# FFN input product by Strassen's method in 18 of 22 pairs, with running sums of the output in DRAM

## The chip, the cores and the metric

One core of a Trainium2 chip runs the whole kernel. The metric is the time of one execution on the device in microseconds; the median of three runs is given, and the profile is of one further execution.

## The reference

An encoder block on 1024 tokens of width 1024: a projection feeds an attention branch and a state-space branch, they are merged, and a gated FFN follows. Only the FFN matters here:

```python
h = _rms(x, g_pre_ffn[l]) * (1.0 + sc2) + sh2
g, up = jnp.split(h @ w_ffn_in[l], 2, axis=-1)
f = (jax.nn.silu(g) * up) @ w_ffn_out[l]
x = x + gt2 * _rms(f, g_post_ffn[l])
```

The hidden width is 2816, which is 22 tiles of 128. `sh2`, `sc2` and `gt2` come from a vector `c` through a 1024x6144 matrix.

## The kernel before, in words

Data lie with channels on the 128 partitions and tokens along the free axis, in two halves of 512 tokens. Products are kept near float32 accuracy by splitting both operands into a high part (fp32r, a cast on ScalarE) and a low part (a subtraction on VectorE); `mm3` (L197) then makes three matmuls for each 128x128 block of weights: high by high, high by low, low by high. Instructions stand on each engine in the order in which the program emits them.

A pair is one tile of 128 hidden channels: its gate columns and its up columns of the input weights. `ffn_in` (L1599) gets both weight tiles (128x1024, 8 blocks of k), makes for each half two sums of 8 x 3 matmuls of 512 columns, so 96 a pair over both halves, then Silu on ScalarE, a multiplication on VectorE, and the split of the result into `fhi` and `flo`. `ffn_out` (L1616) makes one output tile (128 channels by one half, m of 8) from the pairs of one group: 3 matmuls a pair, then adds PSUM to the running sum `facc` (tile `mr`), which stays in SBUF. `FGROUPS` (L31) gives the pairs of each group, 4, 4, 4, 4, 3 and 3. The first and the last group run half by half, so that work for the other half can lie beside them; the others run both halves for each weight tile.

`WStream` (L150) issues weight loads on SyncE (L166) in the order of use, at most two raw tiles, and splits them one tile ahead of the use (`get`, L188). `prod` (L1477) calls `tick` every other k, which emits one step of a generator from `backlog`: the norm of the other half in `chain` (L1531) before the FFN, and `final` (L1628), which after the last sums norms them, adds the residual and stores the result. `ada_load` and `ada_do` (L927, L937) load rows of the 6144-column matrix and reduce each with one VectorE operation of 128x1024 (L455); eight of these, for the last gate, stand in the FFN loop (L1666), one in attention at step 2. The last output half is made in quarters of 256 columns. `ps_b` (L1372) gives one of 8 PSUM banks.

A DMA is issued by an instruction on the queue of SyncE, ScalarE or GpSimd. Where its target or source buffer is still in use, that instruction waits, and what is behind it on the queue waits too.

## Time and profile before

| | |
|---|---|
| median of 3 runs | 1685.14 us (1682.86 to 1685.48) |
| profiled execution | 1684.47 us |
| its span, first to last instruction | 1682.7 us |
| mean granted clock of TensorE | 0.983 |
| busy: TensorE / VectorE / ScalarE / GpSimd | 1618.4 / 977.7 / 552.5 / 164.0 us |
| moved by DMA | 189.66 MB |

The FFN begins near 930 us and lasts to the end. Busy time of TensorE is modelled, and its matmuls overlap: the time that one costs is read from the starts of a run of them. "Idle before" gives what a waiting instruction was released by. Timeline rows give start, duration, engine, line, operation and tile; "x2" after a row means that so many of a kind were merged.

### The profile page before, as it was taken

Reading aid. Unit: us, or ns where it says so; the run is one execution under the profiler, and the core shown is the slowest. Engines: PE = TensorE matmul, PEld = TensorE weight load, DVE = VectorE, ACT = ScalarE, POOL = GpSimd, SP = SyncE. Lnnn points to the kernel's source line nnn. Section 1 sums busy time; section 2 is a strip of 40 time slices with the busy share of each in tenths; the row PEclk is TensorE's granted clock in tenths of the full one; section 3 lists DMA queues with packets and bytes.
Section 4 is the critical chain, followed back from the end, with each engine's and each line's share of the span. In section 5 each row is a group of like instructions: output and inputs, shape, how many; then the busy total and the mean of one; then the engine's idle time right before and its main releaser. Section 6 shows DMA issues by size and latency. Waiting matters only on the chain.

```text
span 1682.7 us, 19415 instructions
## 1 busy us (share of the span) xinstructions
PE 1618.4 (96%) x7454; PEld 1309.0 (78%) x7454; DVE 977.7 (58%) x1615; ACT 552.5 (33%) x743; POOL 164.0 (10%) x221
## 2 busy tenths in 40 slices
PE   6989999999899999999999999999999999999995
PEld 6878888888688677767777778888888888888874
DVE  6978898977857778854636763223223222323366
ACT  4142322223531467763334443211111121121233
POOL 0430000012220000000524200000000000000002
PEclk9899999999999999999999999999999999999998
DMA  8143333567987424202523442212111111111243
GB/s 330 63 124 100 108 103 94 157 218 221 310 244 223 104 63 101 45 14 67 196 94 107 162 135 91 73 66 79 59 63 51 50 51 50 51 41 48 80 142 129
DMA packets 90748, 189.66 MB, mean 113 GB/s; under 512 B 19992, under 2 KB 36504, under 8 KB 90656
## 3 DMA queue, kind: packets, MB, share of 16 engines
q1 hardware_dynamic: 57920, 120.62, 23.7%
q10 hardware_dynamic: 27104, 49.95, 8.6%
q0 software_dynamic: 5632, 17.86, 3.5%
q8 instruction: 58, 0.95, 0.2%
q14 instruction: 34, 0.28, 0.1%
HBM read 148.61 MB, written 39.78 MB: 112 GB/s over the span
## 4 chain that ended last, share of the span: by engine, by line
PE 65%; DVE 20%; ACT 5%; DMA 4%; issue 4%; ACTq 1%; SPq 0%; DVEq 0%; POOLq 0%
PE mm L203 17%; PE mm L202 17%; PE mm L201 17%; DVE t L66 5%; DVE wlo L66 2%; PE sc L1255 1%; PE sc L1256 1%; PE sc L1257 1%; PE pv L1281 1%; PE pv L1280 1%; PE pv L1282 1%; ACT whi L183 1%; DMA mxd<-mneg 1%; PE mx L1203 1%; DVE s L695 1%
## 5 line engine op out<-in xcount | busy, mean ns | idle before, releaser
L202 PE MATMUL mm<-mh,whi 128*128 128x512 f32 x736 | 289.3, 393 | 4.8 <-DVE mh L74 3.1
L201 PE MATMUL mm<-mh,whi 128*128 128x512 f32 x736 | 289.8, 394 | 0.8 <-ACT mh L1404 0.5
L203 PE MATMUL mm<-mh,wlo 128*128 128x512 f32 x736 | 288.7, 392 | 1.7 <-DVE wlo L66 1.6
L66 DVE TENSOR_TENSOR wlo<-wraw,whi 128x1024 fp32r<-128x1024 f32 (+1 forms) x128 | 155.8, 1235 | 80.2 <-ACT whi L183 80.1
L66 DVE TENSOR_TENSOR silu<-mm,silu 128x512 f32<-128x512 f32 x44 | 30.4, 692 | 277.4 <-PE mm L203 271.2
L183 ACT CAST whi<-wraw 128x1024 fp32r<-128x1024 f32 (+1 forms) x128 | 129.9, 1036 | 149.0 <-PE mm L202 137.0
L202 PEld LDWEIGHTS mm<-mh,whi 128*128 128x128 f32 x736 | 139.2, 189 | 38.2 <-DVE mh L74 6.6
L203 PEld LDWEIGHTS mm<-mh,wlo 128*128 128x128 f32 x736 | 139.2, 189 | 32.9 <-DVE wlo L66 4.3
L201 PEld LDWEIGHTS mm<-mh,whi 128*128 128x128 f32 x736 | 139.2, 189 | 31.1 <-ACT whi L183 0.9
L201 PE MATMUL mm<-hhi,whi 128*128 128x512 f32 x384 | 156.7, 408 | 1.5 <-ACT ev L604 1.5
L202 PE MATMUL mm<-hlo,whi 128*128 128x512 f32 x384 | 152.8, 398 | 1.4 <-DVE hlo L74 1.4
L203 PE MATMUL mm<-hhi,wlo 128*128 128x512 f32 x384 | 153.5, 400 | 0.0
L201 PE MATMUL mm<-fhi,whi 128*128 128x512 f32 x304 | 118.8, 391 | 0.0
L202 PE MATMUL mm<-flo,whi 128*128 128x512 f32 x304 | 118.5, 390 | 0.0
L203 PE MATMUL mm<-fhi,wlo 128*128 128x512 f32 x304 | 118.3, 389 | 0.0
L66 DVE TENSOR_TENSOR mr<-mm,mr 128x512 f32<-128x512 f32 (+1 forms) x88 | 56.3, 641 | 97.1 <-PE mm L203 97.0
L66 DVE TENSOR_TENSOR plo<-p,phi 128x1024 fp32r<-128x1024 f32 x64 | 78.3, 1224 | 40.0 <-ACT phi L1261 39.6
L1613 ACT CAST fhi<-silu 128x512 fp32r<-128x512 f32 x44 | 27.3, 621 | 222.2 <-DVE silu L66 222.2
L201 PEld LDWEIGHTS mm<-hhi,whi 128*128 128x128 f32 x384 | 73.3, 191 | 19.6 <-ACT ev L604 1.9
L202 PEld LDWEIGHTS mm<-hlo,whi 128*128 128x128 f32 x384 | 73.1, 190 | 18.5 <-DVE hlo L74 1.8
L1260 ACT ACTIVATE p<-sc 128x1024 f32<-128x1024 f32 x64 | 65.7, 1026 | 64.5 <-PE sc L1257 64.5
L203 PEld LDWEIGHTS mm<-hhi,wlo 128*128 128x128 f32 x384 | 73.0, 190 | 17.9 <-DVE wlo L66 0.2
(524 smaller groups left out, 2938.7 us busy)
## 6 DMA issues: line engine op xcount, KB each, us to landing
wraw<-in_wfi SPq DMA_DIRECT2D x58, 512.0 KB
wraw<-in_win SPq DMA_DIRECT2D x26, 512.0 KB
wraw<-in_wfo SPq DMA_DIRECT2D x20, 512.0 KB
gdram<-ev ACTq DMA_DIRECT2D x32, 256.0 KB
wada<-in_wada POOLq DMA_DIRECT2D x15, 512.0 KB, 4.3
wraw<-in_wmix SPq DMA_DIRECT2D x10, 512.0 KB
xT<-in_xT SPq DMA_DIRECT2D x8, 512.0 KB
pw<-in_wadk SPq DMA_DIRECT2D x8, 512.0 KB
```

The source lines that it names most:

```text
L66: return self.eng.tensor_tensor(o, a, b, op=op)
L183: A_.copy(hi, t)
L201: PE.matmul(ps, whi[:, c], rhi, start=first, stop=False)
L202: PE.matmul(ps, whi[:, c], rlo, start=False, stop=False)
L203: PE.matmul(ps, wlo[:, c], rhi, start=False, stop=last)
L695: V.tensor_tensor_scan(t[64:P, 511::-1], r[64:P, ::-1], z[i][64:P, ::-1], 0.0, op0=ALU.mult, op1=ALU.add)
L1203: PE.matmul(pieces[j], qt["qhi"][b][0:96, t * P:(t + 1) * P], qt["khi"][b][0:96, halves[j]], start=True, stop=True)
L1255: PE.matmul(ps[:, c], kh[0:97, kc], qh[0:97, c], start=True, stop=False)
L1256: PE.matmul(ps[:, c], kh[0:96, kc], ql[0:96, c], start=False, stop=False)
L1257: PE.matmul(ps[:, c], kl[0:96, kc], qh[0:96, c], start=False, stop=True)
L1260: A_.activation(p, ps, AF.Exp)
L1613: A_.copy(fh[:, c], t)
```

## The change

The gate and up weights of a pair and the two halves of k form a 2x2 matrix of blocks, and the two halves of k and of the tokens another. From pair 4 on, `pair7` makes their product from 7 products of blocks (4 blocks of k by 512 tokens, so 4 x 3 = 12 matmuls each) where 8 were made, with sums of blocks on both sides. The sums of the token side (T1 to T4) are made and split once, in steps from `backlog` (`tops_12`, `tops_4`, `tops_3`); those of the weights are made for each pair by three or four GpSimd operations, and all seven weight blocks are split (`Blocks`). `Blocks.load` issues weight loads on GpSimd's queue, and `Blocks.get` has blocks split three ahead of the use.

Groups become 4, then seven of 2, then 4 pairs. Group 0 runs half by half as before with the old product. Running sums live in a DRAM tensor `fd` [2, 8, 128, 512]: `f_load` brings one tile of 256 KB into one of four buffers `fio`, `ffn_out` adds PSUM to it and stores it back, both on SyncE. In groups 1 to 7 the load of the tile three further on is emitted ahead of the tile itself. The last group makes its sums into SBUF, half 0 and then half 1 in quarters. The eight late reductions move from the FFN to steps 50 to 59 of attention.

```diff
-FGROUPS = [4, 4, 4, 4, 3, 3]
+FGROUPS = [4, 2, 2, 2, 2, 2, 2, 2, 4]
+AHEAD = 3
...
+            ada_do()
+        if 50 <= i < 60:
+            ada_do()
+            ada_load(1, ap, "wada", 2)
...
     ff_es = ExitStack()
-    fp = pool("fp", stack=ff_es)
+    fp = pool("fp", bufs=2, stack=ff_es)
+    mhc = pool("mhc", stack=ff_es)
+    fd = dram.tile([2, KD, P, HF], F32, name="fd")
...
+    def f_load(h, m, c0=0, n=HF):
+        t = f_tile()[:, 0:n]
+        SY.dma_start(t, fd[h, m][:, c0:c0 + n])
+        fio.append(t)
+
+    def ffn_out(g, m, h, w, off, c0=0, n=HF):
         ps = ps_b()[:, 0:n]
-        tiles = ft_group[g]
         c = slice(h * HF + c0, h * HF + c0 + n)
-        prod(ps, w, lambda k: tiles[k][0][:, c], lambda k: tiles[k][1][:, c], FGROUPS[g], m % 2 * FGROUPS[g])
-        r = facc[h][:, m, c0:c0 + n]
-        if g == 0:
+        tiles = [ft[p] for p in range(starts[g], starts[g + 1])]
+        prod(ps, w, lambda k: tiles[k][0][:, c], lambda k: tiles[k][1][:, c], FGROUPS[g], off)
+        if g == last:
+            r = facc[h][:, m, c0:c0 + n]
+            tt(r, ps, fio.pop(0), ALU.add)
+            return r
+        if g:
+            r = fio.pop(0)
+            tt(r, ps, r, ALU.add)
+        else:
+            r = f_tile()
             A_.copy(r, ps)
-        else:
-            tt(r, ps, r, ALU.add)
-        return r
...
+    class Blocks:
+
+
+        def __init__(self, seq):
+            self.seq, self.n, self.got, self.raw, self.hl = seq, 0, 0, [], []
+            self.loads = []
+            for kind, i, j in seq:
+                if kind == "A11":
+                    self.loads += [a["wfi"][2 * i], a["wfi"][2 * i + 1]]
+                elif kind == "O" and j % 2 == 0:
+                    o = 2 * starts[i] * P
+                    self.loads.append(a["wfo"][j:j + 2, :, o:o + HF].rearrange("m p c -> p m c"))
+                elif kind == "L":
+                    o = 2 * starts[i] * P
+                    self.loads.append(a["wfo"][j, :, o:o + D])
+
...
+        def load(self, n=1):
+            for _ in range(n):
+                if self.loads:
+                    t = wp.tile([P, D], F32, name="wraw", tag="wraw", bufs=2)
+                    src = self.loads.pop(0)
+                    G.dma_start(t.rearrange("p (m c) -> p m c", m=2) if len(src.shape) == 3 else t, src)
+                    self.raw.append(t)
...
+        def split(self, src, out=None):
+            hi, lo = out or self.new(src.shape[1])
+            A_.copy(hi, src)
+            tt(lo, src, hi.bitcast(F32), ALU.subtract)
+            self.done.append((hi, lo))
+
+        done = []
+
+        def advance(self, n):
+
+            while self.n < min(n, len(self.seq)):
+                kind, i, j = self.seq[self.n]
+                self.n += 1
+                lo, hi = halves
+                if kind == "A11":
+                    g, u = self.g, self.u = self.raw.pop(0), self.raw.pop(0)
...
+                    self.s1, self.s2 = half_tile(c2, "xk", NXK), half_tile(c2, "xk", NXK)
+                    G.tensor_tensor(self.s1, u[:, lo], u[:, hi], op=ALU.add)
+                    G.tensor_tensor(self.s2, self.s1, g[:, lo], op=ALU.subtract)
+                    G.tensor_tensor(u[:, lo], g[:, lo], u[:, lo], op=ALU.subtract)
+                elif kind == "S2":
+                    self.split(self.s2)
+                elif kind == "S1":
...
+        def get(self):
+            self.advance(self.got + 1 + self.ahead())
+            self.got += 1
+            return self.done.pop(0)
+
+        def ahead(self):
+
+            return AHEAD if self.got < len(self.seq) - 5 else 2
+
+    KINDS = ("A11", "S2", "S1", "S3", "A12", "A22", "S4")
+    seq = []
...
+    for g in range(1, last + 1):
+        seq += [(x, p, 0) for p in range(starts[g], starts[g + 1]) for x in KINDS]
+        seq += [("O", g, j) for j in range(4)] if g < last else [("L", g, j) for j in range(4)]
+    bl = Blocks(seq)
+
...
+    def tops_3():
+
+        v = mos[1]
+        top_new("T3", row_big(0, F32R))
+        for j in range(4):
+            t = half_tile(c2, "ht")
+            stt(t, v[:, 4 + j, :], dsh[:, j:j + 1], v[:, j, :], ALU.add, ALU.subtract)
+            t_split(t, "T3", j)
+            yield
...
+    def pair7(p, prep):
+
+        (h0, l0), (h1, l1) = h2t[0], h2t[1]
+        b11, b21 = ((h0[:, k:k + 4, :], l0[:, k:k + 4, :]) for k in (0, 4))
+        b22 = h1[:, 4:8, :], l1[:, 4:8, :]
+        lo, hi = halves
+
+        def prod7(x):
+            ps = ps_b()
+            sprod(ps, bl.get(), x)
+            return ps
+
+        p1, u2, u3 = half_tile(c2, "ht"), half_tile(c2, "sq"), half_tile(c2, "acc1", 1)
+        gl, uh = half_tile(c2, "acc0", 1), half_tile(c2, "rs", 1)
+        A_.copy(p1, prod7(b11))
+        tt(u2, prod7(tops["T2"]), p1, ALU.add)
+        ps5 = prod7(tops["T1"])
+        prep()
+        tt(u3, prod7(tops["T3"]), u2, ALU.add)
+        tt(uh, ps5, u3, ALU.add)
+        tt(u2, ps5, u2, ALU.add)
+        tt(gl, prod7(b21), p1, ALU.add)
+        A_.activation(gl, gl, AF.Silu)
+        tt(p1, prod7(tops["T4"]), u3, ALU.add)
+        tt(gl, gl, p1, ALU.mult)
+        ft_put(p, lo, gl)
+        tt(u2, prod7(b22), u2, ALU.add)
+        A_.activation(u2, u2, AF.Silu)
+        tt(u2, u2, uh, ALU.mult)
+        ft_put(p, hi, u2)
 
...
+    QF = HF // 2
+    dsh = const.tile([P, 4], F32, name="dsh")
+    tt(dsh, sh2[:, 4:8], sh2[:, 0:4], ALU.subtract)
+    for kind, i, hs in units:
+        h = hs[0]
...
+            if h and m == 4:
+                bl.load(2)
+            if h and m == 6:
+                bl.advance(4)
+    drain()
+    backlog.append(tops_3())
+    for g in range(1, last + 1):
+        big_first = g % 2 == 0
+        for n, p in enumerate(range(starts[g], starts[g + 1])):
+            if (n < 2) == big_first:
+                if n % 2 == 0:
+                    ft_big(1, p)
+            else:
+                ft_new(p)
+            pair7(p, drain if p == starts[1] else tick)
+        if g == last:
+            break
+        order = [(m, h) for m in range(KD) for h in range(2)]
+        for m, h in order[:3]:
+            f_load(h, m)
+        for e, (m, h) in enumerate(order):
+            if m % 2 == 0 and h == 0:
+                w = [bl.get() for _ in range(1)][0]
+            if e + 3 < len(order):
+                f_load(order[e + 3][1], order[e + 3][0])
+            ffn_out(g, m, h, w, m % 2 * FGROUPS[g])
+
...
+    tt(gg2, ada[:, 40:48], g_post2, ALU.mult)
+    facc = [big(F32) for _ in range(2)]
+    x1s = big(F32)
+    slab = big(F32R).rearrange("p k c -> p (k c)")
+    bl.out = lambda: (slab[:, 0:D], slab[:, D:2 * D])
+    for m in range(KD):
+        later(x1s[:, m, :], x1d[m][:, halves[1]])
```

## Rows read from the trace of the kernel before

**Rows 1.** Busy time by stretch: attention, and nearly all of the FFN.

```profile
core 0: us, PE busy (x) PEld busy (x) DVE busy (x) ACT busy (x) POOL busy (x), PEclk, DMA share, GB/s
570.00:790.00 220.00, 213.73 (x908) 161.20 (x907) 155.20 (x141) 142.88 (x147) 3.43 (x7) 0.99 0.21 46
930.00:1590.00 660.00, 658.17 (x2890) 540.88 (x2888) 228.77 (x306) 145.84 (x195) 14.82 (x15) 1.00 0.22 72
```

**Rows 2.** Timeline of VectorE in an output group of 4 pairs.

```profile
1160.77 0.69 DVE L66 TENSOR_TENSOR mr<-mm,mr 128x512 f32<-128x512 f32 x1 [2.03 <-PE mm L203]
1163.49 0.69 DVE L66 TENSOR_TENSOR mr<-mm,mr 128x512 f32<-128x512 f32 x1 [2.03 <-PE mm L203]
```

**Rows 3.** Timeline of TensorE in the last quarter.

```profile
1662.87 0.28 PE L203 MATMUL mm<-fhi,mh 128*128 128x256 f32 x1
...
1663.59 0.28 PE L203 MATMUL mm<-fhi,mh 128*128 128x256 f32 x1
...
1670.36 1.22 PE L266 MATMUL mm<-rs,ones 128*128 128x256 f32 x2 [2.98 <-DVE rs L66]
```

**Rows 4.** Groups by line and shape: busy us, mean ns of one, idle before.

```profile
L66 DVE TENSOR_TENSOR mr<-mm,mr 128x512 f32<-128x512 f32 x72 | 49.7, 691 | 95.3 <-PE mm L203 95.3
L1504 POOL TENSOR_TENSOR acc<-acc,sq 128x512 f32<-128x512 f32 x28 | 40.7, 1461 | 103.7 <-ACT sq L1498 93.5 <-issue 10.0
...
L455 DVE SCALAR_TENSOR_TENSOR wada<-wada,sil 128x1024 f32<-128x1024 f32 x24 | 29.3, 1220 | 10.0 <-DMA wada<-in_wada 10.0
L1613 ACT CAST fhi<-silu 128x512 fp32r<-128x512 f32 x44 | 27.3, 621 | 222.2 <-DVE silu L66 222.2
...
L66 DVE TENSOR_TENSOR mr<-mr,rs 128x512 f32<-128x512 f32 x24 | 21.9, 914 | 4.3 <-ACT rs L1642 2.5 <-ACT rs L1545 1.8
```

**Rows 5.** Waits of SyncE's queue: us in total, times, longest.

```profile
SPq L751 <- DMA kdram<-kk: 15.6, 11, 3.0
```

**Rows 6.** Timeline of SyncE's queue in the state-space branch.

```profile
160.79 1.73 SPq L748 DMA_DIRECT2D kdram<-kk  x4
164.65 3.90 SPq L751 DMA_DIRECT2D tz<-kdram  x8
```

**Rows 7.** Timeline of ScalarE and its queue: stores of 256 KB from three buffers.

```profile
99.57 0.41 ACTq L605 DMA_DIRECT2D udram<-ev  x1
...
102.71 0.59 ACT L604 COPY ev<-mm 128x512 f32<-128x512 f32 x1 [1.07 <-DMA udram<-ev]
...
106.43 0.59 ACT L604 COPY ev<-mm 128x512 f32<-128x512 f32 x1 [3.13 <-DMA udram<-ev]
```

**Rows 8.** By tile and line: ns min/median/max, first and last start.

```profile
L147 ACTq DMA_DIRECT2D out_xt<-mr x24: 338/344/587, 1628.9 to 1677.7; - x24
...
L1811 SPq DRAIN  x3: 7/7/7, 1679.7 to 1682.1; - x3
```

**Rows 9.** The chain that ended last: start, us, what.

```profile
779.85 1.41 DMA sd<-rc
...
961.05 3.02 DMA xk<-in_xT
```

**Rows 10.** DMA issues by line on the page: KB each, us to landing.

```profile
wada<-in_wada POOLq DMA_DIRECT2D x15, 512.0 KB, 4.3
```

**Rows 11.** Busy time by stretch: around a stand-still of TensorE, and early loads.

```profile
825.00:830.00 5.00, 2.81 (x11) 1.40 (x9) 4.56 (x7) 2.81 (x4) 5.00 (x4) 1.00 0.00 2
830.00:835.00 5.00, 4.38 (x11) 3.02 (x10) 3.06 (x2) 2.02 (x3) 0.78 (x1) 0.50 0.36 112
835.00:840.00 5.00, 5.00 (x19) 3.99 (x18) 0.00 (x0) 0.46 (x1) 0.00 (x0) 0.82 0.28 97
30.00:35.00 5.00, 5.00 (x21) 4.48 (x22) 4.47 (x10) 0.00 (x0) 0.00 (x0) 1.00 1.02 402
```

**Rows 12.** Timeline of VectorE at the end of a group's last pair.

```profile
1152.68 0.69 DVE L66 TENSOR_TENSOR silu<-mm,silu 128x512 f32<-128x512 f32 x1 [8.81 <-PE mm L203]
1154.06 0.69 DVE L66 TENSOR_TENSOR flo<-silu,fhi 128x512 fp32r<-128x512 f32 x1 [0.69 <-ACT fhi L1613]
```

More of the change, by code (lines that the diff above doesn't have):

```diff
@@ L136, in _body @@
     ada = const.tile([P, 48], F32, name="ada")
-    sil = const.tile([P, D], F32, name="sil")
+    sil_es = ExitStack()
+    sil = pool("sil", side="right", stack=sil_es).tile([P, D], F32, name="sil")
     pending = []
@@ L290, in _body @@
     units = []
-    for g, n in enumerate(FGROUPS):
-        for hs in ((0,), (1,)) if g in (0, last) else ((0, 1),):
-            units += [("in", p, hs) for p in range(starts[g], starts[g + 1])] + [("out", g, hs)]
+    for hs in ((0,), (1,)):
+        units += [("in", p, hs) for p in range(FGROUPS[0])] + [("out", 0, hs)]
     wl = [(a["win"][i], KD * P) for i in range(26)]
@@ L303, in _body @@
             wl += [(a["wfi"][2 * i], KD * P), (a["wfi"][2 * i + 1], KD * P)]
-        elif i < last or hs == (0,):
-            c = 2 * FGROUPS[i] * P
-            wl += [(a["wfo"][m, :, 2 * starts[i] * P:2 * starts[i] * P + c], c) for m in range(KD // 2)]
+        else:
+            c = 2 * FGROUPS[0] * P
+            wl += [(a["wfo"][m, :, 0:c], c) for m in range(KD // 2)]
     win = WStream(wp, wl, D, (2, 3))
@@ L1576, in chain @@
         low(*prev)
-    mos = [row_big() for _ in range(2)]
+    mos = [row_big(i) for i in range(2)]
     sqs = [Squares(c2, half_tile(c2, f"acc{h}", 1), G) for h in range(2)]
@@ L1616, in ffn_out, with ft_new, ft_big, ft_put @@
-    def ffn_out(g, m, h, w, c0=0, n=HF):
+    def ft_new(p):
+        ft[p] = tuple(fp.tile([P, S], F32R, name=n, tag=n) for n in ("fhi", "flo"))
+    def ft_big(i, p):
+        t = row_big(i, F32R).rearrange("p k c -> p (k c)")
+        for j in range(2):
+            ft[p + j] = t[:, 2 * j * S:(2 * j + 1) * S], t[:, (2 * j + 1) * S:(2 * j + 2) * S]
+    def ft_put(p, c, t):
+        fh, fl = ft[p]
+        A_.copy(fh[:, c], t)
+        tt(fl[:, c], t, fh[:, c].bitcast(F32), ALU.subtract)
+    def ffn_in(p, h):
+        wg, wu = win.get(), win.get()
+        if not h:
+            if p < 2:
+                ft_new(p)
+            elif p == 2:
+                ft_big(0, p)
+        c = halves[h]
+        pg, pu = ps_b(), ps_b()
+        hi, lo = h2t[h]
+        for w, ps in ((wg, pg), (wu, pu)):
+            prod(ps, w, lambda k: hi[:, k, :], lambda k: lo[:, k, :], KD)
+        t = half_tile(c2, "acc0", 1)
+        A_.activation(t, pg, AF.Silu)
+        tt(t, pu, t, ALU.mult)
+        ft_put(p, c, t)
@@ new lines, in tops_4 @@
+    def tops_4():
+        (h0, l0), (h1, l1) = h2t[0], h2t[1]
+        tops["T4"] = h1[:, 0:4, :], l1[:, 0:4, :]
+        h2, l2 = tops["T2"]
+        for j in range(4):
+            t, u = half_tile(c2, "ht"), half_tile(c2, "sq")
+            tt(t, h0[:, 4 + j, :].bitcast(F32), h2[:, j, :].bitcast(F32), ALU.subtract)
+            G.tensor_tensor(u, l0[:, 4 + j, :].bitcast(F32), l2[:, j, :].bitcast(F32), op=ALU.subtract)
+            yield
+            tt(t, t, u, ALU.add)
+            yield
+            t_split(t, "T4", j)
+            yield
@@ new lines, in _body @@
+    tt(gg2, ada[:, 40:48], g_post2, ALU.mult)
[3 more added lines that the diff above has]
+    bl.out = lambda: (slab[:, 0:D], slab[:, D:2 * D])
+    for m in range(KD):
+        later(x1s[:, m, :], x1d[m][:, halves[1]])
+    out_w = {}
+    for h, c0, n in ((0, 0, HF), (1, 0, QF), (1, QF, QF)):
+        sq = Squares(c2, half_tile(c2, "acc0" if h == 0 else "acc1", 1)[:, 0:n], V)
+        for m in range(3):
+            f_load(h, m, c0, n)
+        for m in range(KD):
+            if h == m % 2 == 0:
+                out_w[m // 2] = bl.get()
+            if m + 3 < KD:
+                f_load(h, m + 3, c0, n)
+            r = ffn_out(last, m, h, out_w[m // 2], m % 2 * FGROUPS[last], c0, n)
+            sq.add(r)
+            A_.activation(r, r, AF.Copy, scale=gg2[:, m:m + 1])
+        fin = final(h, c0, n, sq, half_tile(c2, "rs", 1))
+        if h and c0:
+            next(fin)
+            for _ in range(TN):
+                tick()
+            next(fin)
+        drain()
+        backlog.append(fin)
```

162 lines of the change are left out of this document (82 added, 80 removed).

## The prediction, made before the change was run

> **What bounds the kernel now.** I read the stages first (busy time by stretch), because the change sits in one of them. From 930 to 1590 us, nearly the whole FFN, TensorE is busy 658 of 660 us at granted clock 1.00 while VectorE has 229, ScalarE 146 and GpSimd 15 [rows 1]. So the FFN is bound by the number of matmuls, and everything else there is cover. The price of a matmul is not its listed 390 ns, since they overlap: in the timeline the adds of two following output tiles, 12 matmuls of 512 columns each, start 2.72 us apart [rows 2], so one costs 2.72/12 = 0.2267 us. With 256 columns, six of them go from 1662.87 to 1663.59, 0.12 us each [rows 3]. Other groups only price the new work: what a VectorE, ScalarE and GpSimd operation takes [rows 4], and how long a store or load lasts from its issue until the next instruction may go [rows 5 to 10].
>
> **Removed: matmuls.** Of 22 pairs, 18 take 7 products of 12 matmuls (4 blocks of k, 3 each) for 96: 84. That is 18 x 12 = 216 fewer, x 0.2267 = **-49.0 us**, all on the path. The last output group has 4 pairs instead of 3, and its second half runs in quarters of 256 columns: 24 matmuls of 512 become 48 of 256, 48 x 0.12 - 24 x 0.2267 = **+0.3 us**.
>
> **Added beside the products.** A pair now lasts 84 x 0.2267 = 19.0 us of TensorE. VectorE gets 7 splits and 11 combining operations of 128x512, some 0.69 us each [rows 4]: 18 x 0.69 = 12.4 us. ScalarE gets 12 of about 0.6 us, GpSimd 4 of 1.46 us [rows 4]. Weights are split three blocks (3 x 2.72 = 8.2 us) ahead, and the two 512 KB loads are issued on GpSimd's queue some 11 us before the next pair's first product; such a load lands in 4.3 us [rows 10]. I take all this at nothing while TensorE runs; it would cost if VectorE came late, which is the next part.
>
> **Added: the running sums through DRAM.** This is the part that I think decides. Groups 1 to 7 have 2 pairs, so an output tile is 6 matmuls, 1.36 us, and the 16 tiles of such an output phase are 21.8 us. Each tile now needs a 256 KB load and a 256 KB store, both issued by SyncE in this order: load of tile e+3, then store of tile e. There are 4 buffers, so the load of tile e+3 takes the buffer of tile e-1 and must wait until the store of e-1 has *landed*. Queued behind that waiting load on SyncE is the store of e. So stores go out no faster than one per c = (store, issue to landing) + (issue of a load, about 0.4 us). SyncE does sit like this now: it waited 11 times for stores to kdram [rows 5].
>
> How long a store takes has no row of its own; bounds: a store of small rows landed in 1.41 us and is the far end [rows 9]; the last 128 KB output store starts at 1677.7 and SyncE is past all of them at 1679.7, 2.0 us [rows 8]; four 15 KB stores issued from 160.79 for 1.73 us, the last near 162.2, free a load at 164.65, 2.4 us [rows 6]; a 256 KB store in 512-byte rows issued at 99.57 frees its buffer at 102.71, 3.1 us [rows 7]. I take 2.5 us: the 128 KB store is nearest, with as much again to move and a load issued just ahead of it. So c = 2.9 (2.4 to 3.5). A 256 KB load took 3.0 us with its issue [rows 9]; I take 2.8. The Trainium skill, "DMA: Bandwidth & Descriptors", section "Anatomy of one DMA", gives a fixed 2.0 us plus bytes/436e3 for GpSimd's path, most of it the receipt of the write; an estimate from it is 2.6 us for 256 KB, c = 3.0 and a loss 8 us larger than mine; the 2.0 us row agrees in kind.
>
> Now one output phase from its start. The first add ends at 1.36 + 0.2 + 0.69 = 2.25 us and four loads are there already. From tile 4 on, add e ends at 2.25 + (e-4)c + store + load + 0.69; for e = 15: 2.25 + 31.9 + 2.5 + 2.8 + 0.69 = 40.1 us. PSUM has 8 banks, so the matmuls of the phase go on beside this. But VectorE takes its work in program order, and behind add 15 stands the split of the fourth weight block (S3) of the next pair, which three-ahead issues only with that pair's first product: ready at 40.8. TensorE wants it after 21.8 + 3 x 2.72 = 29.9. It waits 10.9 us; seven such phases, **+76 us** (33 at c = 2.4 with a load of 2.6, 128 at c = 3.5 with one of 3.0).
>
> After TensorE stood still for some 4 us, its granted clock was 0.50 (1.2 of 2.4 GHz) in the next 5 us and 0.82 in the 5 after; 11 and 19 matmuls ran where 22 do at 1.00 [rows 11]. Less the idle part that is some 2 us per stall, 7 x 2 = **+14 us** (0 to 24).
>
> **Moved.** Eight reductions of 1.22 us [rows 4] go from the FFN, where VectorE had room, into attention, where it has 155 of 220 us busy [rows 1]. A step there is 220/64 = 3.4 us and the loads take 4.3 [rows 10], so VectorE may sit up to 0.9 us in each: 0 to 7, I take **+2 us**. The 44 operations that make the sums T1 to T4 run under products, nothing. At the end the whole norm of half 0 must fit under half 1's output (192 x 0.12 = 23 us); of its 29 steps only 16 are paced under the first quarter, the rest is put out at once: some 12 VectorE operations of 0.91 us [rows 4] = 11 us beside 11.5 us of TensorE, then the last adds. The end from the last matmul to the spread of the norm is 1663.6 to 1670.4 now [rows 3]; **+5 us** (0 to 8).
>
> **Sum**, against the profiled execution's 1684.5 us (span 1682.7 and 1.8 around it; the median 1685.1 is 0.6 above): -49.0 + 0.3 + 76 + 14 + 2 + 5 = +48, **1733 us**. With c = 2.4 and a clock cost of 7: 1683. With c = 3.5 and the upper ends: 1684.5 - 49 + 128 + 24 + 7 + 8 = 1803.
>
> **Rivals.** *The saving stays* (the other side). If stores land within some 1.7 us, or SyncE doesn't hold the next store behind them, the adds keep near TensorE and S3 is in time. For it: the 1.41 us store [rows 9], and a phase's 16 x 512 KB at the 402 GB/s seen once [rows 11] take 21 us, just the phase. Left are -49, the moved parts +7, and a short stall at each group's end: from the last product to the second half's flo pass an add, Silu, product, cast and subtraction, now 1152.68 to 1154.75 from the product on [rows 12], with 1.3 us more for add and Silu 3.4 us, against 2.3 us of other matmuls; 7 x 1.1 = 8. 1684.5 - 49 + 7 + 8 = 1650. The point from which it decides is where stall plus clock equals 42 us, 6 us a phase, c of about 2.4. *Worse*: transfers queue behind each other (the other stores of that run freed their buffers later than the first [rows 7]). At c = 4.5 a phase gives 2.25 + 49.5 + 4.1 + 4 + 1.4 - 29.9 = 31 us of wait, x 7 = 219: 1684.5 - 49 + 219 + 14 + 7 = 1876. *In between*: c of 2.2 to 2.4, 1660 to 1685, at its upper end no change that can be told.
>
> **Chances.** Forecast (1685 to 1803) 0.58; saving stays (1640 to 1660) 0.26; worse 0.10; in between 0.06. About 0.2% is what a measurement here can tell from no change. Faster 0.29, same 0.03, slower 0.68. Range 1644 to 1803: it takes in the faster rival and leaves out the worse one. The forecast's own range is 1685 to 1803.
>
> **What would show it.** If right: matmuls fall by 216 and their spacing stays; in each output phase of groups 1 to 7, stores leave SyncE 2.4 to 3.5 us apart and loads wait on stores, while adds fall behind the matmuls; TensorE idles about 8 to 15 us near the fourth product of the next pair, its releaser the split wlo on VectorE, and the granted clock drops after it. If wrong: stores follow at 1.4 to 2 us and TensorE is busy throughout; then the time falls to about 1650. What would make it wrong in size is the landing time of a store between loads, which no row of this trace shows: 0.1 us of it is 12 x 0.1 x 7 = 8 us.

## The result, and the profile after

The changed kernel takes 1870.9 us (median of 4 runs, 1867.5 to 1872.0) against 1684.0 us for the kernel before, run beside it: ratio 1.111, 95% interval [1.1085, 1.1136]. It is slower, as forecast, but by 187 us where I had 48, and outside my range. Below, a ratio is always to the kernel before on the same chip, and a time worked out from it is the ratio times 1684.0.

The matmuls fell as reckoned: the page of before lists 7454 instructions on TensorE and the page of after this many (PE is TensorE; busy us, share of the span of 1870.0 us, instructions). The difference is 192 = 216 removed less 24 added by the quarters.

```profile
PE 1633.5 (87%) x7262; PEld 1294.8 (69%) x7262; DVE 1170.1 (63%) x1926; ACT 603.4 (32%) x873; POOL 297.3 (16%) x351
```

TensorE is idle for 236 us of the span, and 153 of them lie between 930 and 1785, in the FFN that had 658 of 660 us busy [rows 1]. The busy time by stretch in one output phase of the changed kernel and the pair after it (columns as in [rows 1]) shows where. The phase starts at 1206.83.

```profile
1206.80:1228.60 21.80, 17.75 (x64) 13.11 (x63) 10.98 (x16) 5.40 (x10) 5.27 (x5) 0.84 0.38 111
1228.60:1263.90 35.30, 18.95 (x74) 14.17 (x72) 8.79 (x14) 1.62 (x3) 0.00 (x0) 0.84 0.54 162
1263.90:1296.30 32.40, 32.40 (x130) 26.50 (x131) 19.30 (x27) 9.23 (x16) 8.95 (x9) 0.91 0.31 106
```

In the second stretch TensorE is busy for about half the time, and the DMA engines move 162 GB/s, far from the 402 of [rows 11]: no engine is full there, everybody waits. The waits from 930 to 1870 us say for whom (us in total, times, longest):

```profile
SPq L1646 <- DMA fd<-fio: 240.7, 91, 4.1
DVE fio L67 <- DMA fio<-fd: 218.5, 80, 3.8
PE mm L205 <- DVE wlo L67: 96.4, 21, 9.9
PE mm L203 <- DVE fio L67: 19.3, 13, 2.1
PE mm L203 <- ACT fhi L1618: 15.6, 9, 2.5
PE mm L247 <- DVE acc L1508: 14.4, 2, 12.6
```

It is the chain that I forecast: SyncE's queue waits to issue loads until stores have landed, VectorE's adds wait for those loads, and TensorE waits for a weight split that stands behind the adds on VectorE. The chain is only longer than I had it. SyncE's queue in that phase (start, us, what):

```profile
1231.25 0.38 SPq L1664 DMA_DIRECT2D fd<-fio  x1
1234.50 0.32 SPq L1646 DMA_DIRECT2D fio<-fd  x1
1234.92 0.38 SPq L1664 DMA_DIRECT2D fd<-fio  x1
1238.02 0.32 SPq L1646 DMA_DIRECT2D fio<-fd  x1
1238.44 0.38 SPq L1664 DMA_DIRECT2D fd<-fio  x1
```

From a store to the load that waits for it are 3.1 to 3.25 us, then 0.42 us to the next store: over the phase stores leave 3.58 us apart. The first store of the phase frees its buffer later, after 4.3 us, with a 512 KB weight load issued just ahead of it:

```profile
1215.30 0.54 POOL L1688 DMA_DIRECT2D wraw<-in_wfi  x1 [6.70 <-DVE wlo L67]
1215.64 0.32 SPq L1664 DMA_DIRECT2D fd<-fio  x1
1219.93 0.32 SPq L1646 DMA_DIRECT2D fio<-fd  x1
```

VectorE in the same phase (start, us, what, in brackets idle before and what ended it):

```profile
1210.96 0.68 DVE L67 TENSOR_TENSOR sq<-mm,sq 128x512 f32<-128x512 f32 x1
...
1213.71 0.69 DVE L67 TENSOR_TENSOR mr<-sq,mr 128x512 fp32r<-128x512 f32 x1 [0.68 <-ACT mr L1618]
...
1214.92 1.49 DVE L67 TENSOR_TENSOR fio<-mm,fio 128x512 f32<-128x512 f32 x2
...
1223.15 0.69 DVE L67 TENSOR_TENSOR fio<-mm,fio 128x512 f32<-128x512 f32 x1 [1.53 <-DMA fio<-fd]
1226.71 0.69 DVE L67 TENSOR_TENSOR fio<-mm,fio 128x512 f32<-128x512 f32 x1 [2.87 <-DMA fio<-fd]
...
1262.53 0.69 DVE L67 TENSOR_TENSOR fio<-mm,fio 128x512 f32<-128x512 f32 x1 [2.92 <-DMA fio<-fd]
1263.14 1.28 DVE L67 TENSOR_TENSOR wlo<-wraw,whi 128x512 fp32r<-128x512 f32 x2
```

The first add starts 8.1 us after the phase, add 4 ends at 17.0, add 15 at 56.4, and at once behind it comes the split of S3. TensorE's two long waits of the phase, for S1's split behind add 11 and for S3's behind add 15:

```profile
1249.54 0.79 PE L205 MATMUL mm<-T,wlo 128*128 128x512 f32 x1 [4.14 <-DVE wlo L67]
1263.88 0.80 PE L205 MATMUL mm<-mr,wlo 128*128 128x512 f32 x1 [9.85 <-DVE wlo L67]
```

From one output phase to the next are 89.7 us on average (six intervals, 1117.58 to 1655.52), where two pairs and 16 tiles of matmuls are 2 x 19.04 + 21.77 = 59.9: +29.8 each, and +32.4 in the last. With the 192 matmuls (-48.7), seven phases (+211), what lies ahead of the first block product (+10.2, of which 7.8 ahead of the first output tile), the two pairs of group 1 (+3.9) and the tail (+10.7) the spans differ by 187.

### The profile page after: what moved, and what is told of

Its sections match the earlier page's. It is cut to its first block, busy times and chain, and to the rows that moved or that the text cites. A ratio compares the mean times of both kernels' runs of the same rounds, so it can differ in the third digit from the quotient of the medians.

```text
span 1870.0 us, 20217 instructions
## 1 busy us (share of the span) xinstructions
PE 1633.5 (87%) x7262; PEld 1294.8 (69%) x7262; DVE 1170.1 (63%) x1926; ACT 603.4 (32%) x873; POOL 297.3 (16%) x351
## 4 chain that ended last, share of the span: by engine, by line
PE 30%; DVE 28%; DMA 21%; issue 9%; ACT 7%; POOL 2%; SPq 1%; ACTq 0%; DVEq 0%; POOLq 0%
DMA fd<-fio 11%; PE mm L203 5%; PE mm L205 5%; PE mm L204 5%; DVE wlo L67 5%; DVE t L67 5%; DMA fio<-fd 3%; DVE sq L67 2%; DMA wraw<-in_wfo 2%; ACT whi L1702 2%; ACT whi L185 1%; PE sc L1256 1%; PE sc L1257 1%; PE sc L1258 1%; DMA mxd<-mneg 1%
## 5 line engine op out<-in xcount | busy, mean ns | idle before, releaser
L67 DVE TENSOR_TENSOR wlo<-wraw,whi 128x512 fp32r<-128x512 f32 (+2 forms) x191 | 187.3, 988 | 127.3 <-ACT whi L1702 65.4
L67 DVE TENSOR_TENSOR fio<-mm,fio 128x512 f32<-128x512 f32 x112 | 77.2, 691 | 246.6 <-DMA fio<-fd 218.5
L203 PE MATMUL mm<-mh,whi 128*128 128x512 f32 x448 | 178.7, 399 | 14.3 <-DVE fio L67 13.5
L204 PE MATMUL mm<-mh,whi 128*128 128x512 f32 x448 | 177.7, 397 | 5.0 <-DVE mh L75 2.8
L205 PE MATMUL mm<-mh,wlo 128*128 128x512 f32 x448 | 177.4, 396 | 2.2 <-DVE wlo L67 2.1
L1702 ACT CAST whi<-wraw 128x512 fp32r<-128x512 f32 (+1 forms) x121 | 73.6, 628 | 269.4 <-POOL wraw L1729 175.3
L205 PE MATMUL mm<-mr,wlo 128*128 128x512 f32 (+1 forms) x236 | 99.7, 423 | 65.9 <-DVE wlo L67 65.5
L203 PE MATMUL mm<-mr,whi 128*128 128x512 f32 (+1 forms) x236 | 100.4, 425 | 16.5 <-ACT mr L1618 10.6
L203 PEld LDWEIGHTS mm<-mh,whi 128*128 128x128 f32 x448 | 85.6, 191 | 36.4 <-issue 16.8
L204 PEld LDWEIGHTS mm<-mh,whi 128*128 128x128 f32 x448 | 85.4, 191 | 27.2 <-DVE mh L75 6.3
L204 PE MATMUL mm<-mr,whi 128*128 128x512 f32 (+1 forms) x236 | 98.4, 417 | 1.5 <-DVE mr L67 1.5
L203 PE MATMUL mm<-fhi,whi 128*128 128x512 f32 (+1 forms) x196 | 79.3, 404 | 18.5 <-ACT fhi L1618 15.6
L205 PE MATMUL mm<-T,wlo 128*128 128x512 f32 x144 | 63.2, 439 | 29.3 <-DVE wlo L67 29.1
```

The lines of the kernel that those rows point to most:

```text
L67: return self.eng.tensor_tensor(o, a, b, op=op)
L203: PE.matmul(ps, whi[:, c], rhi, start=first, stop=False)
L204: PE.matmul(ps, whi[:, c], rlo, start=False, stop=False)
L205: PE.matmul(ps, wlo[:, c], rhi, start=False, stop=last)
L1702: A_.copy(hi, src)
```

## Experiments on the sums

The theory: stores are held back on SyncE's queue by the load ahead of them, which waits for a buffer. Rivals: the transfers are slow because they share bandwidth, or TensorE is held by the order of VectorE's work and not by the sums.

**No transfers of sums at all** (the sums are added into four fixed tiles).

```diff
-        SY.dma_start(t, fd[h, m][:, c0:c0 + n])
...
-        SY.dma_start(fd[h, m], r)
```

> Left out: all loads and stores of the running sums; adds go to four fixed tiles, so the output is not the block's. Theory: what is left of the change is the products, their combining and the moved parts. Seven periods of a group lose the wait of 27 us before the fourth product and keep some 5 us of waits at the group's start: 1871 - 7 x 25 = 1696 (1685 to 1712), so even free sums would leave the time above the 1684 of before. Rival (VectorE or the weight splits are the bound, and DRAM only hides it): TensorE goes on waiting for the low parts of weights in each group and the time stays above 1750. Second rival (the products alone keep the saving of 49): 1650 or less.

Ratio 1.0053 [1.002, 1.0086], 1693 us: as expected. So the transfers cost 1871 - 1693 = 178 us in all. And without them the change is still no gain, though 49 us of matmuls are gone; that is taken up below.

**Stores on another queue.**

```diff
-        SY.dma_start(fd[h, m], r)
+        A_.dma_start(fd[h, m], r)
```

> The stores of the running sums are issued by ScalarE instead of SyncE; nothing else changes. Theory (the order on SyncE's queue): in the changed kernel a store waits on SyncE behind a load that waits for the landing of the store before it, so stores leave 3.58 us apart. With stores on another queue only the buffer counts: a buffer goes round in store 3.2 + load 3.2 + add and issues 1.0 = 7.4 us for 4 tiles, 1.85 us a tile. Add 15 of a group then ends some 36 us after the start of the output phase instead of 56, TensorE waits about 7 us instead of 27 in each of seven phases: 1871 - 140 = 1730 (1710 to 1750). Rival (traffic: landing is slow because loads and stores of 512 KB a tile press on each other): stores that may go earlier land later, 5 us and more, the cadence stays above 2.7 us and the time above 1790.

1.0411, 1753 us: between the two, nearer the theory. Two thirds of the cost go. Then ScalarE pays. An issue takes it 0.33 us, but it stands at each store until VectorE's add is done: in the merged rows of its queue four stores with these waits span 4.3 to 5 us, and a weight cast waits behind them.

```profile
1206.35 4.99 ACTq L1664 DMA_DIRECT2D fd<-fio  x4
1211.46 0.62 ACT L1702 CAST whi<-wraw 128x512 fp32r<-128x512 f32 x1 [6.55 <-DMA fd<-fio]
1214.82 4.30 ACTq L1664 DMA_DIRECT2D fd<-fio  x4
```

**The store of a tile ahead of the load of the tile three on**, same queue.

```diff
-            if e + 3 < len(order):
-                f_load(order[e + 3][1], order[e + 3][0])
             ffn_out(g, m, h, w, m % 2 * FGROUPS[g])
+            if e + 3 < len(order):
+                f_load(order[e + 3][1], order[e + 3][0])
```

> Both loads and stores stay on SyncE, but in an output phase the load of the tile three further on is emitted behind the store of the present tile instead of ahead of it. Theory (order on the queue): a store now waits only for the landing of the store two before it, so two stores need 3.6 us, 1.8 us a tile, and the buffer's round of 7.4 us for 4 tiles gives 1.85 us: the same 1730 (1710 to 1750) as with stores on ScalarE's queue. Rival (traffic): no cadence under 2.7 us, time above 1790. Third possibility: if time falls here but not with stores on ScalarE, ScalarE's own waiting work holds the stores.

1.0504, 1769 us: again between the two, 19 us above the theory's range. Stores now leave about 2.2 us apart:

```profile
1213.27 0.38 SPq L1664 DMA_DIRECT2D fd<-fio  x1
1215.21 0.32 SPq L1646 DMA_DIRECT2D fio<-fd  x1
1215.62 0.38 SPq L1664 DMA_DIRECT2D fd<-fio  x1
1217.41 0.32 SPq L1646 DMA_DIRECT2D fio<-fd  x1
```

**Loads two tiles ahead instead of three**, order as in the change; the load then needs the buffer of the store two before.

```diff
-        for m, h in order[:3]:
+        for m, h in order[:2]:
...
-            if e + 3 < len(order):
-                f_load(order[e + 3][1], order[e + 3][0])
+            if e + 2 < len(order):
+                f_load(order[e + 2][1], order[e + 2][0])
```

> The order of load and store on SyncE's queue stays, but the load runs two tiles ahead instead of three; it then takes the buffer of the store two before, not of the one just before. Theory (a store leaves no sooner than a landing after the one whose buffer the load ahead of it needs): two stores are in flight, c = (3.2 + 0.4) / 2 = 1.8, and not below the round of four buffers, (0.7 + 0.4 + 3.2 + 3.2) / 4 = 1.9; with the landings stretched by the overlap, as in the run with the store first, 2.0 to 2.2 us. About 1765 us (1750 to 1775), ratio 1.048. Rival (shorter lead, so each add waits for its load): c at 2.9 or more, 1820 us and above.

1.0498 [1.0469, 1.0526], 1768 us: as expected, from the opposite direction, a shorter lead. Stores leave 2.2 to 2.4 us apart:

```profile
1146.86 0.38 SPq L1664 DMA_DIRECT2D fd<-fio  x1
1148.54 0.32 SPq L1646 DMA_DIRECT2D fio<-fd  x1
1148.95 0.38 SPq L1664 DMA_DIRECT2D fd<-fio  x1
1150.90 0.32 SPq L1646 DMA_DIRECT2D fio<-fd  x1
1151.31 0.38 SPq L1664 DMA_DIRECT2D fd<-fio  x1
```

Three ways of letting two stores be under way at once take away 102 to 118 of the 178 us. So the order on the queue holds the larger part. What remains is, by an estimate, the round of four buffers, (add 0.7 + issue 0.4 + landing 3.2 + landing 3.2) / 4 = 1.9 us a tile, still above the 1.36 us of a tile's matmuls; no run with more buffers was made.

**Half the bytes.** What are the 3.2 us of a landing made of?

```diff
-        SY.dma_start(t, fd[h, m][:, c0:c0 + n])
+        SY.dma_start(t[:, 0:n // 2], fd[h, m][:, c0 // 2:c0 // 2 + n // 2])
...
-        SY.dma_start(fd[h, m], r)
+        SY.dma_start(fd[h, m][:, 0:HF // 2], r[:, 0:HF // 2])
```

> Each load and each store of the sums moves only 256 of the 512 columns (half of every sum is left out, so the output is not the block's); four fixed tiles, the same number of transfers, adds and waits in the same order. It tells what the 3.2 us of a store and of a load are made of. Theory A (nearly all is a fixed time per transfer; bytes at the 400 GB/s that the chip showed are 0.65 us of 256 KB): half the bytes save 0.33 us in each, so 12 x 0.33 + 0.65 = 4.6 us a phase, 7 x 4.6 = 32: about 1839 us, stores 3.25 us apart. Theory B (the transfers share bandwidth with each other and bytes are most of it, some 1.6 us of 3.2): c falls to about 2.0 to 2.3, a phase loses nearly all its stall, 1740 to 1765 us. Rival C (the time does not depend on bytes): 1871.

1.0503 [1.0473, 1.0533], 1769 us: theory B, against my view that a landing is nearly all fixed time.

```profile
1225.87 0.32 SPq L1649 DMA_DIRECT2D fio<-fd  x1
1226.29 0.38 SPq L1667 DMA_DIRECT2D fd<-fio  x1
1228.46 0.32 SPq L1649 DMA_DIRECT2D fio<-fd  x1
1228.88 0.38 SPq L1667 DMA_DIRECT2D fd<-fio  x1
```

Stores leave 2.6 us apart, a store with half the bytes frees its buffer in 2.1 to 2.2 us: 1.0 us less for 128 KB less in it and 128 KB less in the load issued 0.4 us before it. That is 256 KB in 1.0 us, some 260 GB/s. By a line through these two sizes, an estimate, the 3.2 us are about 1.2 fixed and 2.0 that go with the bytes of the store and of the load beside it. Half the bytes take off as much (102 us) as the other order does: the order sets how many landings stand one behind the other, the bytes how long each is, and the two savings don't add.

## Experiments on the first add and on VectorE's order

The first add of a phase ended 8.8 us after its start where I had 2.25. Two causes were open.

**Output weights not loaded**, their splits read a block that lies in SBUF.

```diff
-                elif kind == "O" and j % 2 == 0:
-                    o = 2 * starts[i] * P
-                    self.loads.append(a["wfo"][j:j + 2, :, o:o + HF].rearrange("m p c -> p m c"))
...
-                    self.split(self.raw[0][:, halves[j % 2]])
-                    if j % 2:
-                        self.raw.pop(0)
-                        self.load()
+                    self.split(h2t[0][0][:, j, :].bitcast(F32))
```

> The output weights of groups 1 to 7 are not loaded: their splits read a block that already lies in SBUF (so these products multiply other numbers, the output is not the block's); all else is issued in the same order. In the changed kernel the first add of an output phase starts 8.1 us after the phase, where I had reckoned it done at 2.25, because VectorE stands behind a split that waits for its weight load. Theory (that load makes VectorE late): the first add ends at 2.3 to 3.5 us, each phase gets 5.5 to 6.5 us shorter: 7 x 6 = 42, about 1829 us (1822 to 1835). Rival (VectorE's own chain at the group's end makes it late): 1865 to 1871.

1.0995 [1.0962, 1.1027], 1852 us: half of what the theory gave, and not by its mechanism. In the phase that starts at 1119.1 the first two adds still come 7.1 us later (after: 7.5 in that phase), behind the last pair's own operations:

```profile
1124.96 0.69 DVE L67 TENSOR_TENSOR flo<-sq,fhi 128x512 fp32r<-128x512 f32 x1 [0.68 <-ACT fhi L1618]
...
1126.17 1.28 DVE L67 TENSOR_TENSOR fio<-mm,fio 128x512 f32<-128x512 f32 x2
```

What the run gains lies elsewhere. No weight load is under way beside the first store of a phase, and in five of the seven phases that store frees its buffer after 2.0 us (2.4 and 2.8 in the others) where the changed kernel's takes 4.3:

```profile
1126.88 0.32 SPq L1664 DMA_DIRECT2D fd<-fio  x1
1128.91 0.32 SPq L1646 DMA_DIRECT2D fio<-fd  x1
```

On average add 15 ends 2.2 us earlier, 7 x 2.2 = 15 of the 19 us. The estimate from half the bytes agrees: 1.2 us and 256 KB at 260 GB/s are 2.2 us for a store alone, and with a 512 KB load beside it 4.2.

**The last pair's combination left out.**

```diff
+        if p + 1 in starts and p + 1 <= starts[last]:
+            for n, x in enumerate((b11, tops["T2"], tops["T1"], tops["T3"], b21, tops["T4"], b22)):
...
+                prod7(x)
+            ft[p] = ft[p - 1]
+            return
```

> In the last pair of groups 0 to 7 that the block product makes, its seven products are computed, but their combination into gate and up, the Silu, the product and the two splits are left out (the output reads the pair before it twice, so the output is not the block's). Leaving out the output's weight loads had moved the first add of an output phase only from 8.2 to 7.7 us after the phase's start. Theory (it is that pair's own chain of VectorE and ScalarE operations, which stands ahead of the first add): the first add ends at 2.3 to 3.5 us, the long wait of TensorE in the next pair gets 5 to 6 us shorter, 7 x 5.5 = 38: ratio 1.088, about 1833 us (1825 to 1840). Rival (the first add is late for its sums or for the splits of the next weights): 1860 to 1871.

1.0827 [1.078, 1.0875], 1823 us: the theory, and 48 us where it gave 38, 2 us beyond its range. In the phase that starts at 1126.1 the first add waits only for its matmuls and ends 2.3 us after the start, which is the number of my prediction:

```profile
1127.67 0.69 DVE L67 TENSOR_TENSOR fio<-mm,fio 128x512 f32<-128x512 f32 x1 [0.95 <-PE mm L205]
```

So the lateness is that pair's chain: its last products come 2.72 us apart, and for each VectorE and ScalarE hand a tile to and fro (sum, Silu, product, cast, difference), in program order ahead of the adds. In the phase that starts at 1206.83 VectorE is busy for 5.8 of the 8.1 us before the first add, with that chain and three weight splits, and waits three times 0.7 us for ScalarE.

**The order of the splits.** Twice I tried to take S3's split out from behind add 15.

```diff
-AHEAD = 3
+AHEAD = 4
```

> Weights are split four blocks ahead instead of three (AHEAD = 4), nothing else. In the changed kernel the split of S3, which product 4 of the next pair reads, is put out with that pair's first product, behind add 15 on VectorE. Four ahead puts it out with tile 12, behind add 11, and what then stands behind add 15 is the split of A12, read one product (2.7 us) later. Theory (VectorE's program order makes the wait): each of seven output phases gets 2.7 us shorter, 7 x 2.7 = 19, about 1852 us; and if the weight load behind S4's split, now taken one product earlier, no longer delays the first add of a phase (it starts 8.1 us after the phase does, I had 2.25), up to 5 us a phase more: 1817 to 1852. Rival (the wait is for the sums themselves or for weight loads, whatever the order of splits): 1871 within 5.

1.1205 [1.1176, 1.1235], 1887 us: a miss, slower. The edit brought a wait of its own, so it tells nothing on the theory: the fifth block needs a buffer that the running product still reads, and ScalarE stands on that 14 times (115.9 us in all), with the casts of the pair behind it.

```profile
1231.01 0.62 ACT L1702 CAST whi<-xk 128x512 fp32r<-128x512 f32 x1 [6.53 <-PE mm L204]
```

At S3's place alone the buffer is free earlier, so there the split can be moved by itself:

```diff
                 w = [bl.get() for _ in range(1)][0]
+                if m == 6:
+                    bl.advance(bl.got + 4)
```

> The split of S3, the fourth block of the next pair, is put out with output tile 12, behind add 11 on VectorE, instead of behind add 15; its buffer is free by then, unlike with four ahead, where ScalarE waited for buffers 14 times. Theory (VectorE's program order makes the long wait): the wait goes to the next product, 2.7 us later, and is 2.7 us shorter, 7 x 2.7 = 19: about 1852 us. Rival (the wait is set elsewhere, by TensorE's own lag or by the buffers of the sums): 1866 to 1871.

1.1079 [1.1044, 1.1115], 1866 us: 5 us of the 19, and the interval takes in no change at all. The wait did go to the next product and did shrink by about 3 us:

```profile
1262.01 0.79 PE L205 MATMUL mm<-mh,wlo 128*128 128x512 f32 x1 [6.41 <-DVE wlo L67]
```

but the distance of the phases fell by only 0.7 us on average: add 15 ended 0.6 us later, and there are more small waits for weight casts (10 of them before matmuls on mr, 5.7 us, where the changed kernel has 5, 2.9 us). Whether these took the rest isn't settled. What it does show is that moving one split is worth little while the adds themselves end at 56 us.

## Experiments ahead of the FFN and in the tail

The first output tile starts 7.8 us later than before (973.96, now 981.79). All of it arises in attention, where the eight added reductions stand. Two other queues for their loads:

```diff
-            ada_load(1, ap, "wada", 2)
+            ada_load(1, ap, "wada", 2, SY)
```

> The eight loads for the moved reductions in attention are issued by SyncE instead of GpSimd; nothing else changes. Theory: on GpSimd's queue they stand behind the load of the row maxima, which waits until 744 us for its store; the first reduction then holds VectorE for 13 us and TensorE for 10 (its wait for the low part of the exponentials). On SyncE they go out early: the wait of 10.4 us is gone, 1871 - 9 = 1862 (1858 to 1866). Rival (the reductions themselves load VectorE, whoever issues): the time stays within 3 us of 1871.

1.1207, 1887 us: a miss: nothing gained in attention, and some 16 us more in all, for which I have no cause. In the profiled execution, 10.5 us longer than the changed kernel's, the output phases are no longer than there; the first output tile starts 4.1 us later, and the stretch behind the last pair is 6.7 us longer.

```diff
-            ada_load(1, ap, "wada", 2)
+            ada_load(1, ap, "wada", 2, A_)
```

> The loads of the ada weights in attention are issued on ScalarE's queue, where neither GpSimd's wait for the softmax maximum nor SyncE's slow store of that maximum stands before them. The changed kernel enters the FFN's outputs 8 us later than the one before. Theory (those loads come late because of the queue they stand in): the 8 us come back, about 1863 us, and VectorE's waits for wada in attention vanish. Rival (the added reductions themselves fill VectorE there, or ScalarE, the busiest helper in attention, is late with issuing): 1871 or a few us above.

1.1124 [1.1096, 1.1152], 1873 us: a miss too. But the three traces agree in one row. After the change (GpSimd's queue), the chain of waits and VectorE's timeline:

```profile
732.67 11.08 DMA mxd<-mneg
```

```profile
748.76 1.22 DVE L456 SCALAR_TENSOR_TENSOR wada<-wada,sil 128x1024 f32<-128x1024 f32 x1 [12.95 <-DMA wada<-in_wada]
```

With ScalarE's queue, SyncE's store of the softmax maxima, the load issued 0.8 us after it, and the reduction that waits for that load:

```profile
735.06 0.38 SPq L1211 DMA_DIRECT2D mxd<-mneg  x1
735.90 0.34 ACTq L935 DMA_DIRECT2D wada<-in_wada  x1
749.82 1.23 DVE L456 SCALAR_TENSOR_TENSOR wada<-wada,sil 128x1024 f32<-128x1024 f32 x1 [8.80 <-DMA wada<-in_wada]
```

The load takes 13.9 us instead of the 4.3 of [rows 10]. On GpSimd's queue it isn't issued until that store has landed; on the others it is, and lands no sooner. The Trainium skill, "DMA: Bandwidth & Descriptors", section "Issuing engines are not separate DMA queues", says that DMAs started by different engines run on the same 16 DMA engines; this case agrees, as far as it goes: from SyncE's and from ScalarE's queue the same reduction started at 749.9 and 749.8 us, and from GpSimd's, where the load was issued only at 744.9, at 748.8. So the place in time had to change:

```diff
-        if 50 <= i < 60:
-            ada_do()
+        if 55 <= i < 65:
+            if i > 56:
+                ada_do(1)
             ada_load(1, ap, "wada", 2)
```

> The eight ada reductions stay in attention, but their loads start five steps later and each is issued two steps before its reduction. In the three variants so far, with the loads on GpSimd's, SyncE's and ScalarE's queue, the second reduction started at 748.8, 749.9 and 749.8 us whatever the queue, some 15 us after SyncE had issued the slow store of the softmax maxima; a load issued on ScalarE's queue 0.8 us after that store took 13.9 us. Theory (that store holds up whatever is loaded beside it, and the added loads were put right beside it): with loads after it, attention is as long as before the change and the 8 to 10 us come back: 1861 to 1864 us. Rival (the eight reductions fill VectorE, whenever they run): 1868 to 1873.

1.1057 [1.1029, 1.1086], 1862 us: as expected, 9 us. VectorE's waits for these loads fall from 16.4 to 1.7 us, and the first output tile starts at 975.75.

The tail: TensorE waits between the two quarters of the last output.

```profile
1841.97 1.01 PE L247 MATMUL mm<-ones,acc 128*128 128x1 f32 x4 [12.59 <-DVE acc L1508]
```

Two attempts, more steps of half 0's norm beside the first quarter, and four of its adds on GpSimd:

```diff
+            if h and c0 == 0:
+                tick()
+                tick()
```

> Two more steps of the pending work are put out after each tile of the first quarter of the last output, so that the norm of half 0 (29 steps) runs beside that quarter's matmuls instead of after them. In the changed kernel TensorE waits 12.6 us between the two quarters for VectorE to finish that norm. Theory (the pacing of that work makes the wait): the 12.6 us fall to some 3 to 5, since VectorE has 16 x 0.9 us of it for 11.5 us of matmuls: 1861 to 1864 us. Rival (VectorE's sum of work decides, and steps put between the adds delay these in turn): 1868 to 1871.

```diff
-            if h and (c0 == 0 or m % 2 == 0):
+            if c0 == 0 and h or m % 2 == 0:
```

> Four of the eight residual adds of half 0's final norm go from VectorE to GpSimd. Spreading that norm's steps had taken only 2.5 us from TensorE's 14.5 us of waits in the tail and nothing from the time. Theory (VectorE's sum of work between the quarters makes that wait): 4 x 0.9 us less on VectorE, the wait falls by 3 to 4 us: 1867 us, at the edge of what can be measured. Rival (an add on GpSimd takes 1.3 to 1.5 us and half 0's stores end later): 1871 or above.

1.1105 and 1.111: neither moved the time. The pacing took this wait to 10.1 us, the four adds left it at 12.4. In the changed kernel VectorE is busy for 8.6 us of the wait, mostly with that norm, and waits 3.9 us for loads of xk (the residual). With four adds on GpSimd VectorE is busy for 7.8 us and waits 4.6 for these loads, and GpSimd waits 4.0 for one: that points to the loads, but no run changed them, so why taking work out or ahead didn't shorten the end stays open.

## Together, and what eats the saving

> Three edits at once, everything computed: the store of a sum is issued ahead of the load of the tile three on (alone: ratio 1.050), S3 is split behind add 11, the ada loads start five steps later. Theory (the three costs add up): 1768.7 - 19 - 8 = 1742 us (1735 to 1752). Rival (with the store first, the sums keep near enough that the split's place no longer matters): 1761. Neither beats the kernel before.

Store ahead of load, S3's split early, ada loads late: 1.0454 [1.0425, 1.0483], 1760 us. That is the run with the store first less the 8 to 9 us of attention, the rival: the split's place brings nothing there.

> Four edits, everything computed: loads two tiles ahead, S3 split behind add 11, ada loads five steps later, four adds of the final norm on GpSimd. Theory: as the run of three edits with the store first (ratio 1.0454), less 3 to 4 us in the tail: ratio 1.043, about 1757 us (1747 to 1766). It stays above the kernel before, since even without any transfer of sums the ratio was 1.005.

With loads two ahead instead of the store first, and the four adds on GpSimd besides: 1.0444 [1.0414, 1.0474], 1759 us, as expected, and no better. Nothing with all the work done comes near the kernel before, and the last two runs say why. Both leave the transfers of sums out and load the ada weights late, and the second one leaves the last pair's combination out as well (the edits are those above):

> As the run without any load or store of the sums (four fixed tiles, the output is not the block's), and the ada loads five steps later as well. Theory (what these two cost adds up): ratio 1.0053 - 0.0054 = 1.000, 1684 us (1680 to 1688): with the sums free and attention as before, the 49 us of matmuls are still all spent. Rival (attention's late start had covered something in the FFN): 1692 or above.

0.9967 [0.9949, 0.9985], 1678 us: a little faster than before, 6 us beyond what I expected of it and 2 beyond the range.

> As the run before it, and the combination of the seven products is left out in the last pair of each group (its output reads the pair before it twice). In the run without transfers TensorE still waited 23.7 us at the starts of output phases for that pair's casts and differences (13.1 + 5.6 + 3.0 + 2.0) and some matmuls ran at the lower clock. Theory (the group's end is what eats the rest): 24 us or a little more come back with the clock, ratio 0.984, about 1657 us (1650 to 1663). Rival (TensorE then waits for something else, the weight splits first): 1672 or above.

0.9801 [0.9782, 0.982], 1650 us. Here the FFN is full again, as in [rows 1] (660 us, TensorE busy):

```profile
930.00:1590.00 660.00, 653.72 (x2841) 531.34 (x2841) 372.43 (x537) 194.03 (x314) 145.95 (x137) 1.00 0.20 69
```

So the bill of the change, from run to run: matmuls 1684 - 49 = 1635; tail and what else was not touched, +15 (1650); the chain at the end of seven groups, +28 (1678); attention, +14 (1693); the sums through DRAM, +178 (1871). The parts depend on what else is there: the chain costs 28 us here and 48 with the transfers. The 14 us are uncertain by 6, from the intervals of the two runs, so they don't differ clearly from the 9 found alone.

## Why the prediction was wrong

**Right.** The bound, the price of a matmul and their number (192 fewer); that the sums through DRAM decide; by which chain, and that TensorE would stand before S3's product for VectorE; that products leave VectorE and GpSimd free enough: with no transfers and no group end, TensorE is busy 653.7 of 660 us. After TensorE goes on, the lower clock (0.91 on average there) costs nearly what I took: 46 + 84 matmuls are 29.5 us and lasted 32.4, so 2.9 a phase for my 2.

**The step that failed is "one output phase from its start", in three terms.** I had add 15 ending at 40.1 us; it ended at 56.4.

1. *The first add*: 2.25, measured 8.8, +6.5. I let it follow its own matmuls and priced the end of a group [rows 12] only for TensorE and only in a rival. VectorE runs in program order, so the same chain stood ahead of every add of the phase. I had asked what is queued behind the adds (S3) and not what is queued in front of them. Confirmed by leaving that chain out: the add ended at 2.3.
2. *The first store and load*: 5.3 taken, 4.3 + 3.2 measured, +2.2; a 512 KB weight load, issued by GpSimd at 1215.30, is under way beside that store, which leaves at 1215.64. In the run without loads of output weights no such load is there, and that store took 2.0 us. The prediction had no term for it.
3. *c*: 2.9 taken, 3.58 measured, eleven times: +7.5. A store landed in 3.2 us. The row of a 256 KB store [rows 7] had said 3.1, and I chose the 128 KB store [rows 8] as nearer and added 0.5 for twice the bytes and the load ahead. A 256 KB store alone takes 2.0 us, so what I mis-sized is the transfer beside it: some 1.2 us where I had 0.5. By the Trainium skill's page "DMA: Bandwidth & Descriptors", section "Anatomy of one DMA", whose fit is per DMA and for GpSimd's path, an estimate is 2.6 us for 256 KB: the stores measured here lie on both sides of it, 2.0 us alone and 3.2 with a load beside it.

Together +16.2 a phase, 7 x 16.2 = 113 of the 121 us by which the phases came out above my 76 + 14; the clock's 0.9 a phase is 6 more. With c = 3.5 at the upper end of the range, the first add alone (7 x 6.5 = 45) was enough to leave it: 1803 + 45 = 1848. My rival with c = 4.5 gave 1876, near the measurement, but by a wrong c.

**The moved reductions**: +2 taken, 8 to 9 measured. I priced them by their 4.3 us load [rows 10], and didn't ask what else was in flight when they would be loaded. The bound of 7 was just too low.

**The sums T1 to T4**: put at nothing, since their operations were to run under products. From the first output tile to the first output phase of two pairs the kernel takes 6 us more than the same matmuls took before; TensorE's waits there are 2.8 us, 1.3 of them for T3 (tile `mr`). What the rest is stays open.

**The tail**: +5 (0 to 8), measured +10.7. The drain of half 0's norm was foreseen, but I took it to be mostly hidden. That the wait of 12.6 us is near my 11 us of work is luck: 8.6 us of it are VectorE's work, and 3.9 are waiting for loads, which I hadn't counted.

## What to carry to other kernels

When a transfer through a ring of buffers is issued in order, ask of each issue which earlier transfer its buffer needs: if the answer is "the one just before", the queue has one store under way at a time, here with four buffers. When a chain of adds is to start at a phase's beginning, list what stands ahead of it in its engine's program order, not only what it reads. And fewer matmuls in an FFN that was full pay only if the end of each group (products into splits into the next read) is kept off TensorE's path, which here, with seven groups of two pairs, comes seven times.

## What the runs showed of the hardware

A 256 KB store freed its buffer after 2.0 us with no other transfer under way, after 3.2 us with a 256 KB load issued 0.4 us ahead of it, and after 4.3 us with a 512 KB load issued 0.3 us ahead; with half of the store and of the 256 KB load it was 2.1 to 2.2 us. An estimate of 1.2 us and 260 GB/s for all the bytes under way fits all four within 0.2 us.

A store of 128 x 8 numbers in single 4-byte pieces took 11.08 us, and a 512 KB load issued beside it, on another engine's queue, took 13.9 us instead of 4.3. The load was not shut out: in the run with ScalarE's queue the DMA engines moved 20 GB/s from 736 to 747 us, and 271 from 747 to 750. The Trainium skill's page "DMA: Bandwidth & Descriptors", section "Queues, rings and completion order", has each DMA engine serve the queues with work by turns, by which alone one would expect such a load to be through earlier; no run here shows why it wasn't.
